# Two heads of a tile, issued in turn to the two halves of the TensorE array, in three attentions

## The chip, the cores and the metric

The kernel runs on one core of one Trainium2 chip. The metric is the device time of one execution in microseconds; the time of a kernel is the median of its runs. TensorE (PE in the profile, its weight loads PEld) does the matmuls and writes them to PSUM, which has eight banks of 128 partitions and 512 float32; VectorE (DVE) and ScalarE (ACT) do the elementwise work, GpSimd (POOL) a few powers, SyncE (SP) issues the DMAs. A matmul takes a stationary operand and a moving one; the rows of the array are the partitions over which it sums, the columns are the partitions of its output. A product over 64 partitions uses rows 0-63 or 64-127 of the array, a product with 64 outputs uses columns 0-63 or 64-127.

## What is computed

Three transformer blocks over 512 tokens of 1024 features, in float32, one after the other. Each has projections with large weights, and these hold most of the matmuls. The three attentions that the change touches have heads of 64 features, two of them in the two halves of a tile of 128 partitions:

```python
# block 1, differential attention: 4 heads, two score products each, values 128 wide
a = softmax(q1 k1^T / 8 + bias, causal) - lam * softmax(q2 k2^T / 8 + bias, causal)
out = a v
# block 2, stick-breaking attention: 16 heads of 64
z = q k^T / 8, masked                      # source s before target t
a[s, t] = exp(z[s, t] - sum over s <= u < t of softplus(z[u, t]))
out = a^T v
# block 3, forgetting attention: 8 heads of 64
a = softmax(q k^T / 8 + (cum[t] - cum[s]), causal);  out = a v
```

A fourth attention (block 2, two latent projections, heads of 128 + 64) and a chunked linear attention (block 1) are not touched.

## The kernel before, in words

Activations lie with features on partitions and tokens along the free dimension, a tile being 128 x 512. Projections are made of two float32r numbers an operand, three matmuls a row block (`mm`, L444 to L446; token-major `mm_tok`, L454 to L456), with weights that SyncE loads and ScalarE and VectorE split (`load`). PSUM has a pool of three banks for projections (`pm`) and five banks with roles: `ms` (1), `sc` (2, scores), `tr` (1, transposes), `po` (1, values). A scheduler orders each engine's instructions at build time: what stands first in the program goes first when its operands and a buffer are free; else something later goes ahead. `fill(n)` emits pieces of projection work queued in `fillers` between the steps of an attention, so that TensorE has work while a softmax runs. `later(f, depth)` holds back the value product of a block for `depth` further pieces.

- Differential attention (`diff_attention`): for each head and each block of 128 queries, from the last (512 keys) to the first (128 keys), two score products. `da_proj` has made of q and k, with `stack`, tiles of float32r numbers in which the high parts of one half head stand in its own 64 rows and the low (or again the high) ones in the other 64. `scores` (L423, L424) is one product over 128 rows and one over 64, at least 256 columns wide. Then the softmax of both, one `fill`, and `apply`: transposes, and values at L910.
- Stick breaking (`sb_pair`, eight calls): two heads, the same 64 rows of two tiles (`half`). Source blocks 1, 2, 3 are the first pass, block 0 the second. The five score banks hold blocks 1 and 3 of each head, block 2 of both, block 0 of each head. A product of 64 rows (L1164) is followed by its mask, an identity product over 128 rows in bfloat16 (L1165). Then per bank Abs, Exp, Ln on ScalarE and the split on VectorE and ScalarE; `fill(2)`; the sums over later source blocks (L1182 to L1186), Exp, and values (L1195) into 64 of the 128 output partitions a head. Groups of two calls share a set of five fillers, which the calls' four passes take by twos; the last group has eight gate projections.
- Forgetting attention (`fox_pair`, four calls): first all four query blocks of the head in rows 0-63, then those of the head in rows 64-127. A score product of 64 rows (L1724), its mask (L1725), the softmax, a `fill` at every second block, and `apply` held back by two blocks: transposes (L962), values (L1710) into the head's 64 output partitions. Twelve fillers of the last two calls include two idle turns.

Plain float32 products show as two matmul instructions each in the profile, the high and the low part of the stationary operand.

Of the kernel before, what the change touches and what calls it, by code (L numbers as in the profile page):

```python
# [9 lines left out]
F32 = mybir.dt.float32  # L10
F32R = mybir.dt.float32r
# [5 lines left out]
P = 128  # L17
# [11 lines left out]
# ---------------------------------------------------------------- host layout  # L29
# [201 lines left out]
# ---------------------------------------------------------------- the program  # L231


def idle():
    """a turn that a schedule leaves out"""


class Norm:
    """Takes the tiles of a stage's input as they become final: splits x * g and sums the squares."""
# [20 lines left out]
    def add_pe(self, k, x, sl):  # L260
        """the same with the sums over the tiles on the tensor engine"""
# [19 lines left out]
    def rows(self, sl, role):  # L281
        """the reciprocal root mean squares of some tokens, on all partitions, in PSUM"""
        rc = self.rstd(sl)
        return self.net.bcast_ps([rc[:, j:j + 1] for j in range((sl.stop - sl.start) // P)], role)


class Net:
# [83 lines left out]
    def fill(self, n=1):  # L371
        """emit n of the pieces of work queued to run beside the one at hand"""
# [12 lines left out]
    # ---- operands as sums of two float32r numbers  # L385
# [15 lines left out]
    def stack(self, src, twice, scale=None):  # L401
        """two heads of 64 rows as operands of products over 128 rows: a tile a head with its high parts in its
        own rows and, in the other 64, its low parts, or the high parts again and the low ones apart"""
        nc = self.nc
        tiles = [self.t(F32R, "st") for _ in range(2)]
        low = self.t(F32R, "lo") if twice else None
        for par, hl in enumerate(tiles):
            own, other = ROWS[par], ROWS[1 - par]
            if scale is None:
                nc.scalar.copy(hl[own], src[own])  # L410
                nc.vector.tensor_tensor((low[own] if twice else hl[other]), src[own], hl[own].bitcast(F32), ALU.subtract)
            else:
                nc.scalar.activation(hl[own], src[own], AF.Identity, bias=0.0, scale=scale)
                nc.vector.scalar_tensor_tensor(hl[other], src[own], scale, hl[own].bitcast(F32), ALU.mult, ALU.subtract)
            if twice:
                nc.scalar.copy(hl[other], src[own])
        return tiles, low

    def scores(self, out, a, ca, b, cb, par, start=True, stop=False, **k):
        """out (+)= a[:, ca]^T b[:, cb] of one of two stacked heads; one of a and b is stacked twice"""  # L420
        (at, al), (bt, bl) = a, b
        own = ROWS[par]
        self.nc.tensor.matmul(out, at[par][:, ca], bt[par][:, cb], start=start, stop=False, **k)  # L423
        self.nc.tensor.matmul(out, (al or at[par])[own, ca], (bl or bt[par])[own, cb], start=False, stop=stop, **k)  # L424
# [13 lines left out]
    def mm(self, out, w, c0, x, start=True, stop=True):  # L438
        """out[128 features, tokens] (+)= w[:, c0:c0+128]^T x"""
# [1348 lines left out]
```

## Time and profile before

| | us |
|---|---|
| median of 3 runs | 2565.46 |
| lowest and highest run | 2542.45 and 2569.28 |
| span of the profiled execution | 2572.3 |
| TensorE busy | 2522.8 |
| VectorE busy | 1320.8 |
| ScalarE busy | 1002.6 |
| mean granted TensorE clock | 0.979 |

The span runs from the first to the last instruction of the profiled execution. Busy shares are averages over stages with different limits. Matmuls are pipelined and the ends of their records are modelled, so what a matmul costs is read from its start to the start of the next one.

### The profile page before, as it was taken

Reading aid. Unit: us, or ns where it says so; the run is one execution under the profiler, and the core shown is the slowest. Engines: PE = TensorE matmul, PEld = TensorE weight load, DVE = VectorE, ACT = ScalarE, POOL = GpSimd, SP = SyncE. Lnnn points to the kernel's source line nnn. Section 1 sums busy time; section 2 is a strip of 40 time slices with the busy share of each in tenths; the row PEclk is TensorE's granted clock in tenths of the full one; section 3 lists DMA queues with packets and bytes.
Section 4 is the critical chain, followed back from the end, with each engine's and each line's share of the span. In section 5 each row is a group of like instructions: output and inputs, shape, how many; then the busy total and the mean of one; then the engine's idle time right before and its main releaser. Section 6 shows DMA issues by size and latency. Waiting matters only on the chain. (4 is left out here: it accounts for less than half of the span.)

```text
span 2572.3 us, 31426 instructions
## 1 busy us (share of the span) xinstructions
PE 2522.8 (98%) x12646; PEld 2025.7 (79%) x12646; DVE 1320.8 (51%) x2225; ACT 1002.6 (39%) x1586; POOL 63.5 (2%) x62
## 2 busy tenths in 40 slices
PE   8999999999999999999999999999999999999998
PEld 6857788888888877776777798888896768888887
DVE  7546556774775743345655664223362464532333
ACT  5434433442444445555323533232242444422221
POOL 0000000000000000000000000000010001000001
PEclk9999999999999999999999999999997999999999
DMA  5223235433434331122322123232221111322221
GB/s 189 92 77 96 87 100 179 140 118 120 155 109 131 115 96 59 65 67 73 119 69 83 34 74 110 87 107 98 90 73 51 62 50 42 98 94 96 98 88 52
DMA packets 71746, 240.78 MB, mean 94 GB/s; under 512 B 8232, under 2 KB 11184, under 8 KB 71600
## 3 DMA queue, kind: packets, MB, share of 16 engines
q1 hardware_dynamic: 71600, 238.78, 28.6%
q8 instruction: 99, 1.62, 0.3%
q14 instruction: 47, 0.39, 0.1%
HBM read 236.64 MB, written 2.11 MB: 93 GB/s over the span
## 5 line engine op out<-in xcount | busy, mean ns | idle before, releaser
L444 PE MATMUL pm<-hi,wh 128*128 128x512 f32 (+1 forms) x2736 | 1051.0, 385 | 8.8 <-ACT hi L390 5.0
L445 PE MATMUL pm<-lo,wh 128*128 128x512 f32 (+1 forms) x2736 | 1048.1, 383 | 0.0
L446 PE MATMUL pm<-hi,wl 128*128 128x512 f32 (+1 forms) x2736 | 1043.1, 382 | 0.0
L434 ACT CAST wh<-raw 128x1024 fp32r<-128x1024 f32 (+1 forms) x372 | 382.3, 1029 | 844.4 <-PE pm L445 582.0
L435 DVE TENSOR_TENSOR wl<-raw,wh 128x1024 fp32r<-128x1024 f32 (+1 forms) x372 | 445.1, 1197 | 491.2 <-ACT wh L434 468.6
L444 PEld LDWEIGHTS pm<-hi,wh 128*128 128x128 f32 x2736 | 519.6, 190 | 111.1 <-issue 9.0
L445 PEld LDWEIGHTS pm<-lo,wh 128*128 128x128 f32 x2736 | 519.6, 190 | 100.6 <-issue 7.9
L446 PEld LDWEIGHTS pm<-hi,wl 128*128 128x128 f32 x2736 | 519.3, 190 | 99.1 <-issue 5.5
L454 PE MATMUL pm<-wh,hi 128*128 128x256 f32 x400 | 118.8, 297 | 0.9 <-ACT vt L831 0.9
L456 PE MATMUL pm<-wh,lo 128*128 128x256 f32 x400 | 116.8, 292 | 0.0
L1403 DVE CUSTOM_DVE_ANT_0 adaw<-adaw,cb 128x1024 f32<-128x1024 f32 x72 | 88.0, 1222 | 55.5 <-DMA adaw<-in_w_ada 55.4
L455 PE MATMUL pm<-wl,hi 128*128 128x256 f32 x400 | 116.5, 291 | 0.0
L1482 DVE TENSOR_TENSOR sg<-sg,pm 128x512 f32<-128x512 f32 x44 | 30.2, 687 | 133.3 <-PE pm L446 133.3
L587 POOL TENSOR_TENSOR rc<-ms,nhalf 128x4 f32<-128x4 f32 (+2 forms) x29 | 39.4, 1357 | 2387.1 <-DVE ms L592 1811.1
L454 PEld LDWEIGHTS pm<-wh,hi 128*128 128x128 f32 x400 | 79.9, 200 | 6.4 <-issue 5.1
L456 PEld LDWEIGHTS pm<-wh,lo 128*128 128x128 f32 x400 | 79.8, 199 | 0.8 <-issue 0.6
L455 PEld LDWEIGHTS pm<-wl,hi 128*128 128x128 f32 x400 | 79.9, 200 | 0.6 <-issue 0.2
L496 PE MATMUL pm<-hi,wh 128*128 128x256 f32 (+1 forms) x216 | 61.6, 309 | 10.0 <-ACT hi L397 7.2
L985 DVE SCALAR_TENSOR_TENSOR uy<-ur,vec,uy 128x511 f32<-128x511 f32 x88 | 65.7, 748 | 9.0 <-ACT uy L983 8.0
L258 DVE TENSOR_TENSOR acc<-acc,sq 128x512 f32<-128x512 f32 (+1 forms) x93 | 54.8, 596 | 23.1 <-ACT sq L254 21.9
L498 PE MATMUL pm<-hi,wl 128*128 128x256 f32 (+1 forms) x216 | 66.4, 309 | 0.0
L497 PE MATMUL pm<-lo,wh 128*128 128x256 f32 (+1 forms) x216 | 66.3, 309 | 0.0
(352 smaller groups left out, 2488.4 us busy)
## 6 DMA issues: line engine op xcount, KB each, us to landing
raw<-in_w_gu SPq DMA_DIRECT2D x88, 512.0 KB, 3.4
adaw<-in_w_ada SPq DMA_DIRECT2D x72, 512.0 KB, 3.3
raw<-in_w_dn SPq DMA_DIRECT2D x48, 512.0 KB, 3.3
raw<-in_w_up SPq DMA_DIRECT2D x44, 512.0 KB, 3.3
raw<-in_w_g SPq DMA_DIRECT2D x16, 512.0 KB, 3.3
raw<-in_w_l0qk SPq DMA_DIRECT2D x16, 512.0 KB, 3.4
raw<-in_w_l SPq DMA_DIRECT2D x12, 512.0 KB, 3.4
X<-in_x SPq DMA_DIRECT2D x16, 256.0 KB, 5.8
```

Source lines behind the costliest of these rows:

```text
L434: nc.scalar.copy(wh[:, :n], raw[:, :n])
L435: nc.vector.tensor_tensor(wl[:, :n], raw[:, :n], wh[:, :n].bitcast(F32), ALU.subtract)
L444: self.nc.tensor.matmul(out, a, xh, start=start and k == 0, stop=False)
L445: self.nc.tensor.matmul(out, a, xl, start=False, stop=False)
L446: self.pe = self.nc.tensor.matmul(out, b, xh, start=False, stop=stop and k == n - 1)
L454: self.nc.tensor.matmul(out, xh[:, sl], a, start=start and k == 0, stop=False)
L455: self.nc.tensor.matmul(out, xh[:, sl], b, start=False, stop=False)
L456: self.pe = self.nc.tensor.matmul(out, xl[:, sl], a, start=False, stop=stop and k == len(x) - 1)
L497: self.nc.tensor.matmul(o[:, sl], wh[:, k], xl[:, sl], start=False, stop=False)
L498: self.nc.tensor.matmul(o[:, sl], wl[:, k], xh[:, sl], start=False, stop=k == 7)
L985: nc.vector.scalar_tensor_tensor(y[:, sh:], raw[:, :S - sh], self.v("fconv_w", 44 * (2 - sh) + f), y[:, sh:], mult, add)
L1403: nc.vector.tensor_tensor_reduce(w, w, cb, 0.5, 0.0, ALU.mult, ALU.add, mod[:, i:i + 1])
```

## The change

The two heads of one tile are now issued next to each other, one in rows 0-63 and one in rows 64-127, and their values one in columns 0-63 and one in columns 64-127. In the differential attention `stack` and `scores` go; q and k stay plain float32 tiles, and a score product is one float32 matmul over 64 rows, no wider than its keys. In stick breaking a call takes the two halves of one tile `c`; all products of a pass go out ahead of its masks, block by block and head by head, block 2 of the second head gets a bank of its own (role `ms`), so that Abs, the evacuation and Exp of that tile come in two halves, and the outputs of both heads are copied at once. In the forgetting attention the two heads run together: two score banks a query block, a `fill` at every block, the value products of a pair held back by one pair and issued key block by key block, head by head. Comments and docstrings are removed throughout.

```diff
@@ da_proj
-            y = self.q(F32, "dqk")
+            y = self.t(F32, "dqk")
...
-            (dk if i % 2 else dq).append(self.stack(y, i % 2 == 1))
+            (dk if i % 2 else dq).append(y)
@@ diff_attention
-                for a in range(2):
-                    ps = self.psa("das", "sc")
-                    w = max(n, 2 * P)
-                    self.scores(ps[:, :w], dq[h], slice(qb * P, n), dk[h], slice(0, w), a, stop=True)
+                sc = [self.psa("das", "sc") for _ in ROWS]
+                for ps, r in zip(sc, ROWS):
+                    nc.tensor.matmul(ps[:, :n], dq[h][r, qb * P:n], dk[h][r, :n], start=True, stop=True)
+                for a, ps in enumerate(sc):
@@ stick_breaking
-            for half in range(2):
-                last = self.sb_pair(*cur, half, o[2 * grp:2 * grp + 2], pre)
+            for c in range(2):
+                last = self.sb_pair(*cur, c, o[2 * grp + c], pre)
@@ sb_pair
-        members = [[(1, 0), (3, 0)], [(1, 1), (3, 1)], [(2, 0), (2, 1)], [(0, 0)], [(0, 1)]]
-        roles = ["sc", "sc", "tr", "sc", "sc"]
+        place = {(1, 0): (0, 0), (3, 0): (0, 384), (1, 1): (1, 0), (3, 1): (1, 384), (2, 0): (2, 0), (2, 1): (2, 256), (0, 0): (3, 0), (0, 1): (4, 0)}
+        bank = {(1, 0): (0, 0), (3, 0): (0, 384), (1, 1): (1, 0), (3, 1): (1, 384), (2, 0): (2, 0), (2, 1): (3, 0), (0, 0): (4, 0), (0, 1): (5, 0)}
+        parts = [[(0, slice(0, S))], [(1, slice(0, S))], [(2, slice(0, 256)), (3, slice(256, S))], [(4, slice(0, S))], [(5, slice(0, S))]]
+        roles = ["sc", "sc", "tr", "ms", "sc", "sc"]
...
-        for banks in ((0, 1, 2), (3, 4)):
-            for b in banks:
-                z[b] = self.psa("z", roles[b])
-                for i, (sb, par) in enumerate(members[b]):
-                    zr = reg(z, sb, par)
-                    nc.tensor.matmul(zr, k[par][r, sb * P:(sb + 1) * P], q[par][r, sb * P:], start=i == 0, stop=False, skip_group_check=True)
-                    nc.tensor.matmul(zr[:, 0:P], self.bf["ident"], self.bf["mask_sb"], start=False, stop=False, skip_group_check=True)
+        for tiles, blocks in (((0, 1, 2), (1, 2, 3)), ((3, 4), (0,))):
+            for t in tiles:
+                for b, _ in parts[t]:
+                    z[b] = self.psa("z", roles[b])
+            for sb in blocks:
+                for par, r in enumerate(ROWS):
+                    nc.tensor.matmul(zreg(sb, par), k[c][r, sb * P:(sb + 1) * P], q[c][r, sb * P:], start=sb < 3, stop=False, skip_group_check=True)
+            for t in tiles:
+                for sb, par in [m for m in place if place[m][0] == t]:
+                    nc.tensor.matmul(zreg(sb, par)[:, 0:P], self.bf["ident"], self.bf["mask_sb"], start=False, stop=False, skip_group_check=True)
                 e = self.t(F32, "sbe")
                 with self.tc.issue_after(pre.ins):
-                    nc.scalar.activation(e, z[b], AF.Abs)
+                    for b, sl in parts[t]:
+                        nc.scalar.activation(e[:, sl], z[b][:, width(sl)], AF.Abs)
...
-            for b in banks:
-                for sb, par in members[b]:
-                    col = (sb % 2) * 256 + (2 * par + half) * 64
-                    nc.tensor.matmul(po[64 * par:64 * par + 64, sb * P:], vt[sb // 2][:, col:col + 64], reg(pr, sb, par), start=sb == 1, stop=sb == 0, skip_group_check=True)
-        nc.vector.tensor_copy(out[0][r], po[0:64])
-        nc.scalar.copy(out[1][r], po[64:128])
+            for sb in blocks:
+                for par in range(2):
+                    col = (sb % 2) * 256 + (2 * c + par) * 64
+                    nc.tensor.matmul(po[ROWS[par], sb * P:], vt[sb // 2][:, col:col + 64], reg(pr, sb, par), start=sb == 1, stop=sb == 0, skip_group_check=True)
+        nc.vector.tensor_copy(out, po)
@@ fox_pair
-        def apply(p, qb, par, r):
+        def apply(ps, qb):
...
-            aT = self.transposed(p, qb)
+            aT = [self.transposed(p, qb) for p in ps]
             for kb in range(qb + 1):
-                col = (kb % 2) * 256 + (2 * cl + par) * 64
-                nc.tensor.matmul(po[0][r, qb * P:P * (qb + 1)], vt[kb // 2][:, col:col + 64], aT[:, kb * P:(kb + 1) * P], start=kb == 0, stop=kb == qb)
+                for par, r in enumerate(ROWS):
+                    col = (kb % 2) * 256 + (2 * cl + par) * 64
+                    nc.tensor.matmul(po[0][r, qb * P:P * (qb + 1)], vt[kb // 2][:, col:col + 64], aT[par][:, kb * P:(kb + 1) * P], start=kb == 0, stop=kb == qb)
...
-        for par in range(2):
-            h = 2 * c + par
-            r = slice(64 * par, 64 * par + 64)
-            cb = cum[h]
-            for qb in range(NB - 1, -1, -1):
-                n = P * (qb + 1)
-                ps = self.psa("fxs", "sc")
+        for qb in range(NB - 1, -1, -1):
+            n = P * (qb + 1)
+            sc = [self.psa("fxs", "sc") for _ in ROWS]
+            for ps, r in zip(sc, ROWS):
                 nc.tensor.matmul(ps[:, :n], q[r, qb * P:n], k[r, :n], start=True, stop=False)
+            for ps in sc:
                 nc.tensor.matmul(ps[:, qb * P:n], self.bf["ident"], self.bf["mask_q"], start=False, stop=True)
+            prob = []
+            for par, ps in enumerate(sc):
+                cb = cum[2 * c + par]
...
-                if qb % 2:
-                    self.fill()
-                self.later(lambda p=p, qb=qb, par=par, r=r: apply(p, qb, par, r), 2)
+                prob.append(p)
+            self.fill()
+            self.later(lambda p=prob, qb=qb: apply(p, qb), 1)
```

## Rows read from the trace of the kernel before

**Rows 1.** The page: span, then busy us, share and count of each engine.

```profile
span 2572.3 us, 31426 instructions
PE 2522.8 (98%) x12646; PEld 2025.7 (79%) x12646; DVE 1320.8 (51%) x2225; ACT 1002.6 (39%) x1586; POOL 63.5 (2%) x62
```

**Rows 2.** Windows: from:to, length, busy PE, PEld, DVE, ACT, POOL, clock, DMA, GB/s.

```profile
204.00:351.00 147.00, 146.43 (x689) 109.29 (x687) 90.75 (x237) 65.16 (x137) 6.78 (x4) 1.00 0.27 87
917.00:1203.00 286.00, 286.00 (x1415) 210.35 (x1414) 119.34 (x159) 157.13 (x249) 0.00 (x0) 0.95 0.21 70
1973.00:2137.00 164.00, 161.88 (x959) 119.58 (x959) 88.83 (x256) 72.62 (x152) 3.45 (x5) 1.00 0.18 57
```

**Rows 3.** Timeline, TensorE, stick breaking, first pass: start, length, instruction, count.

```profile
1097.17 0.91 PE L1164 MATMUL z<-sqk 64*128 64x384 f32 x2
1098.01 0.23 PE L1165 MATMUL z<-bf_mask_sb,bf_ident 128*128 128x128 bf16 x1
1098.17 0.48 PE L1164 MATMUL z<-sqk 64*128 64x128 f32 x2
1098.59 0.23 PE L1165 MATMUL z<-bf_mask_sb,bf_ident 128*128 128x128 bf16 x1
...
1101.78 0.36 PE L454 MATMUL pm<-wh,hi 128*128 128x256 f32 x1
```

**Rows 4.** Timeline, TensorE, stick breaking, second pass.

```profile
941.28 1.12 PE L1164 MATMUL z<-sqk 64*128 64x512 f32 x2
...
943.55 0.23 PE L1165 MATMUL z<-bf_mask_sb,bf_ident 128*128 128x128 bf16 x1
943.59 0.48 PE L444 MATMUL pm<-hi,wh 128*128 128x512 f32 x1
```

**Rows 5.** Timeline, TensorE: gating values of two column halves; forgetting values of one head.

```profile
2068.70 1.09 PE L1601 MATMUL sgu<-sw,sv 128*64 128x128 f32 x16
2069.73 0.44 PE L962 MATMUL tr<-cst,fxp 128*128 128x128 f32 x2
...
2081.28 1.09 PE L1710 MATMUL fxo<-aT,fvt 128*64 128x128 f32 x8
2082.29 0.33 PE L962 MATMUL tr<-cst,fxp 128*128 128x128 f32 x1
```

**Rows 6.** Timeline, TensorE, differential attention: two heads' scores of 512, 384, 256 columns.

```profile
279.75 0.48 PE L423 MATMUL das<-st 128*128 128x512 f32 x1
...
281.45 0.50 PE L444 MATMUL pm<-hi,wh 128*128 128x512 f32 x1
...
288.97 0.42 PE L423 MATMUL das<-st 128*128 128x384 f32 x1
...
290.43 0.50 PE L444 MATMUL pm<-hi,wh 128*128 128x512 f32 x1
...
298.31 0.36 PE L423 MATMUL das<-st 128*128 128x256 f32 x1
...
299.54 0.50 PE L444 MATMUL pm<-hi,wh 128*128 128x512 f32 x1
```

**Rows 7.** Timeline, TensorE, differential attention: scores of two heads with projections between.

```profile
323.00 0.42 PE L423 MATMUL das<-st 128*128 128x384 f32 x1
...
325.20 0.33 PE L423 MATMUL das<-st 128*128 128x384 f32 x1
```

**Rows 8.** Tile view of the stacked tiles: count, ns least/median/most, first and last start.

```profile
L410 ACT CAST st<-dqk x16: 602/616/622, 144.1 to 207.4; 64x512 fp32r<-64x512 f32 x16
```

**Rows 9.** Timeline, ScalarE, stick breaking: casts of two banks' high parts.

```profile
1055.85 0.62 ACT L390 CAST hi<-sbe 128x512 fp32r<-128x512 f32 x1 [0.76 <-DVE sbe L1171]
...
1059.05 0.62 ACT L390 CAST hi<-sbe 128x512 fp32r<-128x512 f32 x1 [0.76 <-DVE sbe L1171]
```

**Rows 10.** Windows at half the clock in stick breaking: the first, and all five summed.

```profile
921.30:928.10 6.80, 6.80 (x17) 4.42 (x18) 3.83 (x6) 3.42 (x6) 0.00 (x0) 0.50 0.54 175
sum 27.20, PE 27.20 PEld 19.78 DVE 12.55 ACT 16.75 POOL 0.00; mean PE 5.44 PEld 3.96 DVE 2.51 ACT 3.35 POOL 0.00
```

More of the change, by code (lines that the diff above doesn't have):

```diff
@@ L234, in idle @@
 def idle():
+    pass
 class Norm:
@@ L399, in split_scaled @@
         return h, l
[L401 to L424, printed above, removed]
     def load(self, name, u, kc, g):
@@ L1141, in stick_breaking, with sb_pair @@
         self.out_half("w_l0o", y, norm)
-    def sb_pair(self, q, k, vt, half, out, pre):
+    def sb_pair(self, q, k, vt, c, out, pre):
         nc = self.nc
-        r = slice(64 * half, 64 * half + 64)
-        place = {}
-        for par in range(2):
-            place[1, par] = (par, 0)
-            place[3, par] = (par, 384)
-            place[2, par] = (2, 256 * par)
-            place[0, par] = (3 + par, 0)
-        members = [[(1, 0), (3, 0)], [(1, 1), (3, 1)], [(2, 0), (2, 1)], [(0, 0)], [(0, 1)]]
-        roles = ["sc", "sc", "tr", "sc", "sc"]
-        z, sp, hi, lo, pr = ([None] * 5 for _ in range(5))
+        place = {(1, 0): (0, 0), (3, 0): (0, 384), (1, 1): (1, 0), (3, 1): (1, 384), (2, 0): (2, 0), (2, 1): (2, 256), (0, 0): (3, 0), (0, 1): (4, 0)}
+        bank = {(1, 0): (0, 0), (3, 0): (0, 384), (1, 1): (1, 0), (3, 1): (1, 384), (2, 0): (2, 0), (2, 1): (3, 0), (0, 0): (4, 0), (0, 1): (5, 0)}
+        parts = [[(0, slice(0, S))], [(1, slice(0, S))], [(2, slice(0, 256)), (3, slice(256, S))], [(4, slice(0, S))], [(5, slice(0, S))]]
+        roles = ["sc", "sc", "tr", "ms", "sc", "sc"]
+        sp, hi, lo, pr = ([None] * 5 for _ in range(4))
+        z = [None] * 6
@@ L1157, in sb_pair @@
         reg = lambda tiles, sb, par: tiles[place[sb, par][0]][:, place[sb, par][1]:place[sb, par][1] + S - sb * P]
+        zreg = lambda sb, par: z[bank[sb, par][0]][:, bank[sb, par][1]:bank[sb, par][1] + S - sb * P]
+        width = lambda sl: slice(0, sl.stop - sl.start)
         po, last = None, None
-        for banks in ((0, 1, 2), (3, 4)):
-            for b in banks:
-                z[b] = self.psa("z", roles[b])
-                for i, (sb, par) in enumerate(members[b]):
-                    zr = reg(z, sb, par)
-                    nc.tensor.matmul(zr, k[par][r, sb * P:(sb + 1) * P], q[par][r, sb * P:], start=i == 0, stop=False, skip_group_check=True)
-                    nc.tensor.matmul(zr[:, 0:P], self.bf["ident"], self.bf["mask_sb"], start=False, stop=False, skip_group_check=True)
+        for tiles, blocks in (((0, 1, 2), (1, 2, 3)), ((3, 4), (0,))):
[8 more added lines that the diff above has]
+                    nc.tensor.matmul(zreg(sb, par)[:, 0:P], self.bf["ident"], self.bf["mask_sb"], start=False, stop=False, skip_group_check=True)
@@ L1172, in sb_pair @@
-                sp[b] = e
-                hi[b], lo[b] = self.split(e)
+                for b, sl in parts[t]:
+                    nc.vector.scalar_tensor_tensor(e[:, sl], z[b][:, width(sl)], 0.0, e[:, sl], ALU.max, ALU.add)
+                sp[t] = e
+                hi[t], lo[t] = self.split(e)
             self.fill(2)
-            for b in banks:
-                for sb, par in members[b]:
-                    zr = reg(z, sb, par)
+            for t in tiles:
+                for sb, par in [m for m in place if place[m][0] == t]:
+                    zr = zreg(sb, par)
@@ L1186, in sb_pair @@
                             nc.tensor.matmul(dst, w, reg(lo, src, par), start=False, stop=done, skip_group_check=True)
-                pr[b] = self.t(F32, "sba")
+                pr[t] = self.t(F32, "sba")
                 with self.tc.issue_after(pre.ins):
-                    last = nc.scalar.activation(pr[b], z[b], AF.Exp)
+                    for b, sl in parts[t]:
+                        last = nc.scalar.activation(pr[t][:, sl], z[b][:, width(sl)], AF.Exp)
             if po is None:
                 po = self.psa("sbo", "po")
-            for b in banks:
-                for sb, par in members[b]:
-                    col = (sb % 2) * 256 + (2 * par + half) * 64
-                    nc.tensor.matmul(po[64 * par:64 * par + 64, sb * P:], vt[sb // 2][:, col:col + 64], reg(pr, sb, par), start=sb == 1, stop=sb == 0, skip_group_check=True)
-        nc.vector.tensor_copy(out[0][r], po[0:64])
-        nc.scalar.copy(out[1][r], po[64:128])
+            for sb in blocks:
[3 more added lines that the diff above has]
+        nc.vector.tensor_copy(out, po)
         return last
```

4 lines of the change are left out of this document (1 added, 3 removed).

## The prediction

> **What bounds the kernel now.** I read the page first, for its busy shares: TensorE is busy in 98% of a span of 2572.3 us, VectorE in 51%, ScalarE in 39% [rows 1]. Then the busy time by stretches, for the three attentions that the change touches: the differential attention (204 to 351 us), the stick-breaking attention (917 to 1203) and the forgetting attention (1973 to 2137). The reader is to see that TensorE is busy in all but 0.6, 0 and 2.1 us of them, while VectorE and ScalarE are busy in 42 to 62% and 44 to 55% [rows 2]. Projections queued as fillers run wherever an attention waits for its softmax. So a microsecond of TensorE work that goes is a microsecond of the kernel, as long as the fillers still cover the softmax. Then the order of time, TensorE alone, start to start, because busy times of pipelined matmuls overlap.
>
> **What one score product costs.** In the stick-breaking attention one head and one source block at a time uses 64 rows. 384 columns take 0.84 us until the mask starts, 128 columns take 0.42, and the mask 0.16 until the next product starts [rows 3]. So a product costs 1.64 ns a column ((0.84 - 0.42) / 256) and 0.21 us that do not depend on its length (0.42 - 128 x 1.64 ns): the first weights and the way out of the 64 rows. A mask ahead of a projection costs only 0.04 [rows 4]. One pass over three source blocks of two heads takes 4.61 us [rows 3], the pass over the last block 2.31 [rows 4]; the formula gives 6 x 0.21 + 1536 x 1.64 ns + 5 x 0.16 + 0.04 = 4.62 and 2.30.
>
> **What two halves of the array cost together.** The trace has no two neighbouring products in different rows, but it has them in different columns. Sixteen value products of the spatial gating, issued in turn to columns 0-63 and 64-127, take 1.03 us; eight products of the same 128 columns of data, all of one head of the forgetting attention, take 1.01 [rows 5]. Products in two column halves run wholly side by side, also as float32. For rows the gain is bounded by nothing (each head's stream after the other's) and by the same factor of two. I take two: the scores use separate banks for the two heads, as the new place table of stick breaking shows, and nothing in the column case pays for the second half. The Trainium skill, "TensorE: Matmul & The Clock Gate", section "Measured speedup vs the span model", states 3.07 for four row tiles of 32, not 4; the same share of the ideal would be an estimate of 1.54 for two. The streams below (67.2 us) would then shrink by 23.6 and not 33.6 us, and the time would be 10 us above mine.
>
> **Stick breaking, scores.** Eight calls. The first pass becomes one visit to the 64-row layout: 0.21 + (384 + 256 + 128) x 1.64 ns = 1.47 us, and six masks behind each other. The first of them costs up to 0.16, the others between 0.04 and 0.16; I take 0.4 in all, nearer the low end since no way in or out lies between them (0.24 to 0.96). 4.61 - 1.87 = 2.74. The second pass: 0.21 + 512 x 1.64 ns + two masks 0.2 = 1.25; 2.31 - 1.25 = 1.06. Eight times 3.80 is 30.4 us. At the three places where one group of heads follows another without fillers, the first head's bank comes free before the second's, so the blocks of 384 and 128 columns may go out one head at a time: minus 3 x (512 x 1.64 ns + 0.16) = 3.0. Left: 27.4. The values of the first pass are already issued in column pairs, and the last block's second head waits for its own exponential in either kernel: 0. The added halves of Abs, Exp and evacuation (block 2 now lies in two banks) are ScalarE and VectorE work under the fillers: 0 on the path.
>
> **Forgetting attention.** Before: 32 visits of 0.21 us and 4 pairs x 2 heads x 1280 columns. After: 16 visits, half the stream. 32 x 0.21 + 10240 x 1.64 ns = 23.5 becomes 16 x 0.21 + 5120 x 1.64 ns = 11.8 us, 11.7 less. The masks stay; the way into the 64 rows (0.16 - 0.04 = 0.12, what a mask costs more ahead of a product than ahead of a projection) is taken 16 times less: 1.9. Values: eight in a row take 1.01 us, and as sixteen in turn they take the same for both heads [rows 5]. The groups of a head have 8, 6, 4 and 2 products; at 0.11 a product and 0.15 fixed they cost 1.01, 0.80, 0.58 and 0.36, 2.75 a head, and one of two heads goes in each of four pairs: 11.0. Together 24.6. The transposes stay.
>
> **Differential attention.** The two products over stacked high and low parts become one float32 product a head. Before, two heads of 512, 384 and 256 columns take 1.70, 1.46 and 1.23 us, and the 128-column block is computed 256 wide at the price of 256 [rows 6]: 5.62 a head pair, 22.5 for four. After: 4 x (4 x 0.21 + 1280 x 1.64 ns) = 11.8, and the way into the 64 rows 16 times, 1.9: 8.8 less. In three of the 16 blocks the trace shows the second head 2.2 us behind the first, with projections between, because its bank came free later [rows 7]; there the streams do not meet, which takes back 3 x (384 x 1.64 ns + 0.33) = 2.9. Left: 5.9. The split into stacked tiles goes too: 24 casts of 0.62 us [rows 8] and 16 subtractions, on engines that nothing waited for: 0.
>
> **Where a wait could come.** Both score banks are now taken at once, and the next block's products wait for VectorE to read them. Behind them on TensorE stand the next fillers. In stick breaking one bank's chain to its high part takes 3.2 us (the casts of two banks lie 3.2 apart [rows 9]), so three banks and then two cost about 12 and 9 us a call with scores, exponential and values: 21 x 8 = 168 us against 286 - 27 = 259 us of TensorE work. It stays the bound. For single waits at passes without fillers of their own and at the two idle turns of the forgetting attention I take back 4 us (0 to 15).
>
> **The clock.** Five stretches of the stick-breaking attention, 27.2 us, ran at 0.50 of the clock, 1.2 instead of 2.4 GHz [rows 10]. Each begins within a pass of these 64-row products, one head at a time. That costs 13.6 us. Shorter passes with both halves at work should leave some of them out: I take 6 (-7 to +13.6).
>
> **Sum.** 27.4 + 24.6 + 5.9 - 4 + 6 = 59.9, that is 60 us. 2572.3 - 60 = 2512. The profiled span is 0.3% above the median of the runs (2565.46), so the prediction is 2565 - 60 = 2505 us.
>
> **The rivals.**
> 1. Rows do not overlap, only visits are saved. Stick breaking: 4.61 - (0.21 + 1536 x 1.64 ns + 0.4) = 1.48 and 2.31 - 2.09 = 0.22, times 8: 13.6. Forgetting scores: 3.4 + 1.9 = 5.3, values 11.0. Differential: 22.5 - (3.4 + 16.8 + 1.9) = 0.4. 30 - 4 = 26: 2539 us. For it: no row shows two row halves together; against it: the columns do.
> 2. The chain behind the scores becomes the limit: passes end sooner and fillers run out, so half the gain comes back as waits: 2535. For it: the stretches' fillers are uneven, one of four passes of a group has none of its own. Against it: the 168 us above. The Trainium skill, "TensorEngine Tiling (Array Packing)", section "PSUM Bottleneck", says that tiling speeds up TensorE and not the evacuation; no wait in these stretches shows that yet.
> 3. The order of issue does not survive: if the engine's queue keeps the heads apart as in [rows 7] everywhere, scores cost what they did, and the float32 products of the differential attention cost 32 x 0.33 + 16.8 - 22.5 = 4.9 more: 2570. Against it: only three of 16 blocks there are apart.
> 4. The other side: each of 48 paired steps (16 in each attention) leaves TensorE waiting for both banks. At 2.2 us, the distance in [rows 7] with nothing to fill it, that is 106 - 60 = 46 us more: 2611. It decides from 1.25 us a step (60 / 48). Against it: fillers stand behind nearly every step.
>
> **How the numbers follow.** Forecast 0.64, rival 1 0.13, rival 2 0.11, rival 3 0.05, rival 4 0.07. A change of over 1% (about what a measurement of this kernel can tell; its three runs span 27 us) begins below 2540. The forecast and half of rivals 1 and 2, which end near it, lie there, 0.76; the rest of those and rival 3 within 1%, 0.17; rival 4 above, 0.07. The likeliest case alone: all overlaps, no waits and the whole clock give 60 + 3 + 2.9 + 4 + 7.6 = 77.5 us, 2488; the clock worse by 13 and waits longer by 11 leave 36, 2529. With the scatter of the runs below and rivals 1 and 2 above: 2476 to 2545.
>
> **What would show it.** In the profile after: two score products of different heads starting within some 20 ns of each other; a first stick-breaking pass of about 1.9 us; value groups of the forgetting attention with twice the products in the same time; TensorE still busy throughout the three stretches, which get shorter by some 32, 24 and 6 us (stick breaking with its clock); fewer stretches at 0.50. Wrong it would be if products of different rows started one stream apart (rival 1), if TensorE waited for VectorE at the score banks (2, 4), or if projections stood between the heads (3).

## The result, and the profile after

The changed kernel takes 2527.89 us (median of 4 runs, 2511.96 to 2534.89) against 2556.64 us of the kernel before in the same rounds (4 runs, 2542.45 to 2569.28): ratio 0.9877, 95% interval 0.9832 to 0.9922. It is faster by 1.2%. In a later comparison it was 0.9833 (0.9804 to 0.9863). The predicted 2505 us was 23 us too low; the range, 2476 to 2545, held the time.

The page of the profile after (span; then busy us, share and count of each engine), against [rows 1]:

```profile
span 2510.2 us, 31392 instructions
PE 2456.1 (98%) x12646; PEld 1987.3 (79%) x12646; DVE 1310.9 (52%) x2217; ACT 981.3 (39%) x1570; POOL 62.8 (3%) x62
```

TensorE has lost 66.7 us of busy time with the same 12646 matmuls, and is still busy in 98% of the span. But the two spans, 2572.3 and 2510.2, must not be set against each other as they stand: the granted clock was 0.979 in the one and 0.991 in the other. **Span times mean granted clock** removes this. The four runs of the changed kernel have spans of 2510.2, 2532.3, 2519.9 and 2533.1 us at clocks of 0.991, 0.982, 0.987 and 0.982: the products are 2487.6, 2486.7, 2487.1 and 2487.5. The profile of before gives 2572.3 x 0.979 = 2518. So TensorE's work shrank by 31 us, and the other 31 us between the two profiles are clock. This product, called "at full clock" below, is the measure with which parts of 2 us can be seen. One run's product is rounded by up to 1.3 us, since the clock is given to three digits, and the products of one kernel scatter by some 1.7 us (standard deviation); a mean over four or more runs is good to about 1 us.

Windows of the three stretches after (from:to, length, busy PE, PEld, DVE, ACT, POOL, clock, DMA, GB/s), against [rows 2]:

```profile
208.00:349.00 141.00, 138.97 (x670) 101.83 (x669) 86.28 (x232) 58.86 (x126) 5.93 (x4) 1.00 0.26 85
918.00:1170.00 252.00, 251.63 (x1415) 193.23 (x1414) 119.63 (x167) 152.79 (x259) 0.00 (x0) 1.00 0.25 82
1914.00:2070.00 156.00, 149.37 (x940) 111.77 (x939) 88.16 (x255) 70.36 (x150) 3.46 (x5) 0.97 0.18 60
```

In stick breaking (second row) the same 1415 matmuls take 252 us instead of 286, TensorE is idle for no more than 0.4 us, and the clock is 1.00 instead of 0.95. In the forgetting attention (third row) TensorE is now idle for 6.6 us instead of 2.1, and the clock is 0.97 instead of 1.00.

Timeline of TensorE after (start, length, instruction, count), a first and a second pass of stick breaking, against [rows 3, 4]:

```profile
918.74 1.57 PE L1140 MATMUL z<-sqk 64*128 64x384 f32 x12
920.24 0.51 PE L1143 MATMUL z<-bf_mask_sb,bf_ident 128*128 128x128 bf16 x6
920.56 0.47 PE L419 MATMUL pm<-hi,wh 128*128 128x512 f32 x1
...
936.83 1.13 PE L1140 MATMUL z<-sqk 64*128 64x512 f32 x4
937.89 0.28 PE L1143 MATMUL z<-bf_mask_sb,bf_ident 128*128 128x128 bf16 x2
937.98 0.48 PE L419 MATMUL pm<-hi,wh 128*128 128x512 f32 x1
```

Start to start, the six products of a first pass take 1.50 us and their masks 0.32; before the same work took 4.61. The second pass takes 1.06 + 0.09 instead of 2.31. The tile view of the first 0.4 us of the first pass (count, ns least/median/most, first and last start, form) shows why: two matmuls, one of each head, begin at the same tenth of a microsecond (6 ns apart in the trace) and last 587 ns each, as long as the first matmul of one head alone did before.

```profile
L1140 PE MATMUL z<-sqk x2: 587/587/587, 918.7 to 918.7; 64*128 64x384 f32 x2
```

### The profile page after: what moved, and what is told of

Its sections match the earlier page's. It is cut to its first block, busy times and chain, and to the rows that moved or that the text cites. A ratio compares the mean times of both kernels' runs of the same rounds, so it can differ in the third digit from the quotient of the medians.

```text
span 2510.2 us, 31392 instructions
## 1 busy us (share of the span) xinstructions
PE 2456.1 (98%) x12646; PEld 1987.3 (79%) x12646; DVE 1310.9 (52%) x2217; ACT 981.3 (39%) x1570; POOL 62.8 (3%) x62
```

## The experiments

Every kernel was timed beside the kernel before, in the same rounds. "At full clock" is the mean over its runs. The versions of the last four rows are explained below.

By their times alone the versions with the changed stick breaking can hardly be told from each other: most of their intervals overlap. What follows on parts of a few microseconds rests on the products at full clock and on the traces.

| kernel | median us (runs) | ratio to before, 95% | at full clock, us |
|---|---|---|---|
| before, three comparisons | 2555.77 (13), 2562.97 (13), 2561.78 (11) | | 2519.3, 2517.8, 2518.7 |
| changed | 2527.89 (4) | 0.9877, 0.9832 to 0.9922 | 2487.2 |
| changed, again | 2517.47 (5) | 0.9833, 0.9804 to 0.9863 | 2488.4 |
| stick breaking alone | 2536.71 (4) | 0.9891, 0.9840 to 0.9941 | 2495.8 |
| forgetting attention alone | 2555.51 (10) | 0.9981, 0.9949 to 1.0014 | 2510.2 |
| differential attention alone | 2561.03 (10) | 1.0004, 0.9973 to 1.0036 | 2516.9 |
| score products head by head | 2524.91 (4) | 0.9861, 0.9806 to 0.9916 | 2487.8 |
| second transpose bank | 2530.31 (4) | 0.9880, 0.9828 to 0.9932 | 2479.9 |
| values one step later | 2512.19 (4), 2512.68 (6) | 0.9812, 0.9768 to 0.9857; 0.9812, 0.9771 to 0.9853 | 2475.5, 2474.2 |
| both | 2518.21 (4), 2501.70 (6) | 0.9816, 0.9757 to 0.9874; 0.9783, 0.9745 to 0.9821 | 2473.1, 2471.4 |
| both, without idle turns | 2518.49 (4) | 0.9820, 0.9768 to 0.9871 | 2473.5 |

**One part at a time.** Three kernels take the kernel before and one attention of the changed one. Stick breaking alone:

```diff
-            for half in range(2):
-                last = self.sb_pair(*cur, half, o[2 * grp:2 * grp + 2], pre)
+            for c in range(2):
+                last = self.sb_pair(*cur, c, o[2 * grp + c], pre)
```

> The kernel before, with the stick-breaking part of the change alone. I compare span times mean granted clock (time at full clock), which was 2518 us for the profiled run before and 2487 for each run after. Theory (the parts add up, each is TensorE time that goes): the score products and masks of stick breaking give 25 us, 3 to 4 come back in sums and values, so 2518 - 21.5 = 2497 us at full clock; the clock itself scatters from run to run between 0.980 and 0.991 as in both kernels. Rival (the clock is the gain): the clock stays above 0.990 in all runs, because the passes of single 64-row products are gone, and the median falls by 35 us.

Measured: 2495.8 us at full clock, 22.8 below the mean of before (2518.6), near the 21.5 of the theory. This is most of the whole gain. The clocks of its four runs, 0.983 to 0.991, exclude the rival.

The forgetting attention alone:

```diff
+        for qb in range(NB - 1, -1, -1):
...
+            sc = [self.psa("fxs", "sc") for _ in ROWS]
+            for ps, r in zip(sc, ROWS):
                 nc.tensor.matmul(ps[:, :n], q[r, qb * P:n], k[r, :n], start=True, stop=False)
```

> The kernel before, with the forgetting attention's part of the change alone. Theory: its scores and values give 12 us of TensorE time, of which 2 to 4 come back as transposes, masks and waits: 2518 - 8 = 2510 us at full clock (2507 to 2512). Rival (the differential attention's change gave the rest, this one nothing): 2518, the same as before.

Measured: 2510.2, only 8.4 below before, as expected after the profile, and a third of the 24.6 us predicted. The time itself can't be told from no change.

The differential attention alone:

```diff
...
-                    self.scores(ps[:, :w], dq[h], slice(qb * P, n), dk[h], slice(0, w), a, stop=True)
+                sc = [self.psa("das", "sc") for _ in ROWS]
+                for ps, r in zip(sc, ROWS):
+                    nc.tensor.matmul(ps[:, :n], dq[h][r, qb * P:n], dk[h][r, :n], start=True, stop=True)
```

> The kernel before with the differential attention of the changed kernel alone (one float32 product a head in 64 rows, two heads in turn, no stacked tiles). Theory (the three parts add, so the whole less the two others leaves this one 31.5 - 22.1 - 8.6 = 0.8 us): span times granted clock 2516 to 2518 us against 2518 of the kernel before; a ratio of 1.000 within 0.003. The scores themselves are some 5 us shorter from start to start, and transposes, rows brought to all partitions and projections take it back. Rival (the part is worth the 5.9 us of the prediction, and stick breaking or the forgetting attention lose 5 us in its company): 2512.

Measured: 2516.9, 1.7 below before. 22.8 + 8.4 + 1.7 = 32.9 against 30.7 of the whole (2518.6 less 2487.9, the mean of its nine runs): the parts add, within what the measure can tell, and the rival's loss of 5 us in company is not there.

**Is it the overlap?** In the changed kernel the order of the score products in a stick-breaking pass is turned back to one head after the other; nothing else moves:

```diff
-            for sb in blocks:
-                for par, r in enumerate(ROWS):
+            for par, r in enumerate(ROWS):
+                for sb in blocks:
                     nc.tensor.matmul(zreg(sb, par), ...
```

> The changed kernel with one thing undone: in each stick-breaking pass the three score products of head A are issued first and then the three of head B, instead of A and B in turn. Visits to the 64-row layout, masks behind each other, banks and everything else stay. Theory (the gain is the overlap of neighbours, and TensorE issues in order): only A's last block (128 columns) meets B's first (384); a first pass streams 384 + 256 + max(128, 384) + 256 + 128 = 1408 columns instead of 768, that is 640 x 1.64 ns = 1.05 us more, 8.4 us for the eight calls; the second pass has one block a head and stays. The scores of stick breaking go from 26 to about 34 us; span times granted clock 2495 us instead of 2487. Rival 1 (what paid was the single visit and the masks put together, not the overlap, or the engine finds the pairs itself): nothing changes, first pass 1.8 us, 2487. Rival 2 (rows would overlap even less once the order is broken: all of one head before the other): 768 columns more, 1.26 us a pass, 10 us, 2497.

Measured: 2487.8 at full clock, no difference that can be told in the runs; in the two traces the whole stick-breaking stretch, start to start, is 2.5 us longer (256.9 against 254.5). The passes show something between the theory and rival 1. Timeline of TensorE in this kernel, a pass over three source blocks and one over two:

```profile
916.76 2.32 PE L1140 MATMUL z<-sqk 64*128 64x384 f32 x12
919.01 0.51 PE L1143 MATMUL z<-bf_mask_sb,bf_ident 128*128 128x128 bf16 x6
...
981.00 1.14 PE L1140 MATMUL z<-sqk 64*128 64x384 f32 x8
982.08 0.40 PE L1143 MATMUL z<-bf_mask_sb,bf_ident 128*128 128x128 bf16 x4
```

The pass over three blocks is 2.25 us instead of 1.50; only four of the eight first passes go out in one piece, so this is 3.0 us in all (start to start the scores are 29.1 us instead of 26.1). The pass over two blocks (384 and 128 columns of one head, then of the other) takes 1.08 us, the same as in turn. In the built program all of head A's products of a pass stand ahead of head B's, as written. So products of head B start ahead of products of head A that were issued before them. The tile view of the first 0.75 and 0.84 us of the long pass (count, ns least/median/most, first and last start, forms) shows it:

```profile
L1140 PE MATMUL z<-sqk x3: 376/482/587, 916.8 to 917.5; 64*128 64x384 f32 x2, 64*128 64x256 f32 x1
L1140 PE MATMUL z<-sqk x4: 376/534/587, 916.8 to 917.5; 64*128 64x384 f32 x3, 64*128 64x256 f32 x1
```

A float32 product appears as two matmuls. The order of issue is A 384, 384, 256, 256, 128, 128, then B 384; but the fourth to start, 6 ns behind the first 256 of A, is a third 384: head B's, three matmuls of A ahead of their turn. So strict order, on which the theory's 8.4 us rested, is wrong; overlap is right, because a pass that had none would be 1.26 us longer (rival 2) and this one is 0.75. That the gain came from visits and masks alone is excluded by the pass over two blocks: its 1024 columns at 1.64 ns would take 1.68 us one behind the other. How far ahead B starts differs: with one product of A in between, in the pass over two blocks, B's first starts 13 ns behind A's first; with two in between, in the long pass, it starts 755 ns behind it, together with A's second product.

**Where the forgetting attention's gain went.** Timeline of TensorE in the changed kernel, at the change from one pair of heads to the next:

```profile
1953.41 0.38 PE L937 MATMUL tr<-cst,fxp 128*128 128x128 f32 x2
1953.72 1.12 PE L1702 MATMUL fxs<-fqk 64*128 64x512 f32 x2
1954.77 0.44 PE L937 MATMUL tr<-cst,fxp 128*128 128x128 f32 x2
1955.14 0.43 PE L1691 MATMUL fxo<-aT,fvt 128*64 128x128 f32 x2
1955.50 1.12 PE L1702 MATMUL fxs<-fqk 64*128 64x512 f32 x2
1956.55 0.65 PE L1691 MATMUL fxo<-aT,fvt 128*64 128x128 f32 x6
1957.14 0.28 PE L1704 MATMUL fxs<-bf_mask_q,bf_ident 128*128 128x128 bf16 x2
```

The first head's probabilities are transposed (1953.41), and the second head's must wait until ScalarE has copied them out of the one bank of the role "tr". Into this gap the order of instructions puts what is ready: one head's scores alone (1953.72), and the first value product alone (1955.14), whose partner needs the second copy. Then the other head's scores go alone too (1955.50). In 6 of the 16 score pairs the heads are apart, in four of them with transposes in between like this, and most value groups begin with a single product (two matmuls). Two cures were made. The first puts the values one step later: `self.side` holds work that is done in the next step, behind its transposes.

```diff
         def apply(ps, qb):
+            aT = [self.transposed(p, qb) for p in ps]
+            self.side.append(lambda: values(aT, qb))
+
+        def values(aT, qb):
             if not po:
                 po.append(self.psa("fxo", "po"))
-            aT = [self.transposed(p, qb) for p in ps]
             for kb in range(qb + 1):
```

> The kernel after, but in the forgetting attention the value products of a pair follow one step behind its transposes instead of right behind them. Theory (one transpose bank: the second head's transposes wait for ScalarE to copy the first head's, and single products go out in that gap): the score pairs meet in 15 of 16 blocks instead of 10, values lose the single first products; score products 16.7 to about 12.5 us, values 16.7 to about 12, at full clock 2487 - 9 = 2478 us. Rival (the score banks: the second bank comes free later than the first): the pairs stay apart where they were, 2487 us.

Measured: 2475.5 at full clock, and 2474.2 in a second comparison, beside the changed kernel (2488.4): 12 to 14 us better, with the single bank still in place. The heads are together in 15 of 16 score pairs, as the theory said.

> The version with the values of the forgetting attention one step behind the transposes, beside the changed kernel. Theory (what held the forgetting attention is gone): span times granted clock 2477 +- 2 us in every run, 10 us below the changed kernel; ratio to the kernel before 0.981 to 0.985 against 0.986 to 0.990 of the changed kernel. Rival (the 10 us are an accident of single runs): no difference between the two.

A bank for the second head's transposes, alone:

```diff
-    def transposed(self, p, qb):
+    def transposed(self, p, qb, role="tr"):
...
-        ps = self.psa("tr", "tr")
+        ps = self.psa("tr", role)
...
-            aT = [self.transposed(p, qb) for p in ps]
+            aT = [self.transposed(p, qb, role) for p, role in zip(ps, ("tr", "ms"))]
```

> The changed kernel with one thing altered: in the forgetting attention the second head's probabilities are transposed into a PSUM bank of their own (another role's bank, free at that time), so that they need not wait until ScalarE has copied the first head's out. The values stay where they were, right behind the transposes. Theory (the single transpose bank is what keeps the heads' products apart): most of what the version with the values one step later gained comes by the bank alone, span times granted clock 2478 to 2481 us, against 2487 of the changed kernel and 2477 of that version; start to start scores fall from 16.7 to about 14 us, values from 16.7 to about 14, transposes from 14.1 to about 11. Rival (the place of the values is what counts: they wait for the second copy in any case, and single products of other steps are issued in that gap): 2485 to 2488, with scores and values near 16.7.

Measured: 2479.9, 8 us better, as the theory said. Its details were not: six score pairs are apart as before, which is the rival's point, the scores fell only to 16.2 us, and the transposes, in which a wait of 2.1 us for the copy now lies, stayed at 13.9. The values fell to 14.5 as expected, and the masks from 6.6 to 2.3; in the changed kernel a wait of 3.2 us for the copy lay in them.

Both together, and both without the two idle turns:

> The changed kernel with both cures in the forgetting attention: the second head's transposes in their own bank, and the values one step behind the transposes; the order of fillers stays, with its two idle turns. Theory (both cures take away the same gap): no better than the values' place alone, 2474 to 2478 us in span times granted clock. Rival (each takes away a gap of its own): their gains add, 2468 to 2471. Its difference from the version that also leaves out the idle turns (2474) shows what those turns are worth: within 2 us.

> The version with both cures, beside the two others. Theory (they take away the same gap but for some 4 us): span times granted clock 2472 +- 2 us, ratio to the kernel before 0.979 to 0.983, the lowest of the three. Rival (the second bank gives nothing beyond the values' place): 2477, as the version without it.

```diff
-                self.fillers = [gates[0], idle, gates[1], idle, *gates[2:]]
+                self.fillers = [*gates]
```

> The kernel after, with three edits in the forgetting attention: the second head's transposes go to a bank of their own (role ms), the values follow one step behind, and the fillers of the last two calls lose their two idle turns, so that the branch products stand beside the last blocks. Theory (transposes in one bank plus a tail without fillers): as with the values behind, and of the 6 us of single waits in this stretch half goes too: 2487 - 13 = 2474 us at full clock, median about 2514. Rival (VectorE and ScalarE bound the tail): no better than with the values behind alone, 2478.

Measured: 2473.1 and 2471.4 with both, 2473.5 without the idle turns. The second bank adds 2 to 3 us to the values' place, between the theory and its rival, so the cures take away nearly the same gap. What was expected of leaving out the idle turns is not there: they are worth nothing that can be told. The ratios of the second comparison came out at or below the low end of what was expected (0.9833, 0.9812 and 0.9783). The same change of pairs with both cures, timeline of TensorE:

```profile
1957.69 0.38 PE L937 MATMUL tr<-cst,fxp 128*128 128x128 f32 x2
1958.00 0.87 PE L1694 MATMUL fxo<-aT,fvt 128*64 128x128 f32 x10
1958.80 1.13 PE L1705 MATMUL fxs<-fqk 64*128 64x512 f32 x4
1959.86 0.28 PE L1707 MATMUL fxs<-bf_mask_q,bf_ident 128*128 128x128 bf16 x2
```

The scores of both heads now stand in one row (x4) and take 1.06 us from start to start, where they took 1.05 twice; ten value matmuls go together in 0.80. One of 16 pairs is still apart. The ledger of the stretch, TensorE start to start at full clock, from the first score product to the product behind the last value product; a wait counts for the instruction before it:

| us | before | changed | second bank | values later | both |
|---|---|---|---|---|---|
| scores | 23.5 | 16.7 | 16.2 | 13.8 | 12.2 |
| values | 22.1 | 16.7 | 14.5 | 13.9 | 13.8 |
| transposes | 11.6 | 14.1 | 13.9 | 11.9 | 13.5 |
| masks | 4.5 | 6.6 | 2.3 | 3.8 | 2.1 |
| projections and the rest | 99.2 | 96.2 | 94.9 | 93.2 | 94.7 |
| whole stretch | 160.9 | 150.2 | 141.8 | 136.6 | 136.2 |

With both cures the kernel is 0.9783 (0.9745 to 0.9821) of the kernel before, 2501.70 us in the comparison where the changed kernel took 2517.47 and the one before 2561.78. It is the best version found, though its interval and that of the changed kernel there (0.9804 to 0.9863) still touch.

> The changed kernel once more, beside the two versions with a cure, on one chip in the same rounds. Theory (a kernel's work at full clock is fixed, and the granted clock scatters from run to run): span times granted clock of every run within 2487 +- 2 us, the clock anywhere from 0.979 to 0.992, median 2515 to 2535 us. Rival (the changed kernel holds the clock better than the kernel before, so that part of its gain comes from there): its mean clock over the runs lies above that of the kernel before by more than 0.002.

**The clock.** Measured: products of 2486.3 to 2490.5, a little wider than expected, at clocks of 0.985 to 0.991. Within this comparison the clock went the rival's way, 0.9888 in the mean against 0.9839 of the kernel before; in the first four runs of the changed kernel it was 0.9855, and 0.9853 and 0.9873 in the two kernels beside it here. Over all later comparisons and these four runs, 45 runs with the changed stick breaking had a mean clock of 0.9856, 57 runs without it 0.9845; both sets scatter from 0.979 to 0.992. The difference is worth 3 us, with a 95% interval from 1 us lost to 7 us won, so the time does not show whether the change wins any clock. The 13 kept profiles show where it could. Windows at half the clock: inside stick breaking, one of three and the sum of the three, in each of the two other kernels with the old stick breaking (differential alone, then forgetting alone); and one at L1624, in the kernel before:

```profile
1028.70:1032.10 3.40, 3.40 (x15) 2.76 (x15) 1.58 (x3) 2.38 (x4) 0.00 (x0) 0.50 0.00 0
sum 10.20, PE 10.20 PEld 8.43 DVE 5.74 ACT 7.33 POOL 0.00; mean PE 3.40 PEld 2.81 DVE 1.91 ACT 2.44 POOL 0.00
963.80:970.60 6.80, 6.80 (x29) 5.59 (x28) 3.04 (x5) 4.85 (x9) 0.00 (x0) 0.50 0.00 0
sum 17.00, PE 17.00 PEld 13.57 DVE 8.42 ACT 10.56 POOL 0.00; mean PE 5.67 PEld 4.52 DVE 2.81 ACT 3.52 POOL 0.00
1931.70:1965.80 34.10, 33.95 (x70) 17.25 (x71) 3.04 (x4) 6.22 (x10) 0.00 (x0) 0.50 0.09 31
```

All three profiles with the old stick breaking have 10 to 27 us at 0.50 inside it [rows 10]; of the ten with the new one none has any there. In the profiles this is 5 to 14 us of clock that the change wins in this stretch. But most of the scatter lies elsewhere: 7 of the 13 profiles, with either stick breaking, have a stretch of 31 or 34 us at 0.50 that starts about where the products of L1624 do, which spread the gate sums to all partitions just ahead of the forgetting attention. The change does not touch them. The stretch costs 15 to 17 us, half of what the clock's range from 0.979 to 0.992 is worth. The 31 us of clock between the profiles of before and after are these two: 13.6 from stick breaking and 17 from L1624. All other half-clock stretches sum to 49 us in each.

## Why the prediction was right or wrong

The sign and the mechanism were right, the size was not: without its 6 us for the clock the sum says 54 us, and 31 were measured at full clock. Heads that the order of work keeps apart are what the sum priced too low: the prediction had this as rival 3, at 0.05 and as all or nothing, and allowed for three places in stick breaking, three in the differential attention and none in the forgetting attention; the trace has four, five and six. By the number alone rival 1, at 2539 us, was nearer to the 2528 measured than the forecast, but its mechanism is excluded. Term by term:

- **Overlap of rows: right.** Rival 1 predicted a first pass 1.48 us shorter; it is 2.79 shorter (4.61 to 1.82, predicted 1.87). Its scores take 1.50 us, 1.47 by the full factor of two. The Trainium skill, "TensorE: Matmul & The Clock Gate", section "Measured speedup vs the span model", has 3.07 for four row tiles of 32; the same share of the ideal, an estimate of 1.54 for two, would make them 0.21 + 1536 x 1.64 ns / 1.54 = 1.85 us, which this trace does not show.
- **Stick breaking: 27.4 predicted, 22.8 measured.** Scores and masks fell from 54.8 to 29.7 us (28.0 predicted). Three second passes and one first pass have their heads apart, where a group of heads follows another; three were allowed for. Sums, values and projections became 1.6, 0.9 and 1.1 us longer, which the prediction left out or had at nothing. Why is not shown. The way into the 64 rows, 0.12 us a visit, explains little of it: an instruction other than a mask stands ahead of 22 visits now and stood ahead of 19 of 64 before.
- **Forgetting attention: 24.6 predicted, 8.4 measured.** This is the step that failed: "16 visits, half the stream", and for values "as sixteen in turn they take the same for both heads". Both counted pairs as written in the program. The order on TensorE puts whatever is ready into a wait, and a step had such a wait between its two heads: the second head's transposes wait for the copy out of the one bank, and the values behind them for both copies. Either cure takes most of it away, so it is this wait and not the bank alone. The prediction wrote "the transposes stay": it counted their time and not their bank. Of the evacuation it wrote that no wait in these stretches shows it yet; but the waits of TensorE before have one there, of the values for the copy of the transposes (line, waited for, total, times, longest):

```profile
PE fxo L1710 <- ACT aT L964: 1.2, 1, 1.2
```

  With both cures the stretch is 24.7 us shorter than before (160.9 to 136.2), close to the term, but this is in part luck. The scores gave 11.3 of 11.7 us and the masks 2.4 of 1.9; the values gave 8.3 of 11.0, the transposes became 1.9 longer, and 4.5 lie in projections and the rest. Of these, some 2 come back behind the stretch, which holds ten projection matmuls fewer, at 0.23 us; so it is in the changed kernel's stretch, with nine fewer.
- **Differential attention: 5.9 predicted, 1.7 measured.** The scores themselves fell by 5.4 us (21.8 to 16.4). But five of 16 blocks have the heads apart, not three, and transposes, broadcasts, values and reversals became 3.0 us longer. In the kernel with this part alone the projections became 1.0 us longer, and TensorE waits 1.0 us in this stretch for a DMA, where it waited for none before. The way into the 64 rows was priced at 1.9 us; that the 3.0 are this way is not shown. Timeline of TensorE after, one block with the heads together and one with them apart:

```profile
278.71 1.13 PE L913 MATMUL das<-dqk 64*128 64x512 f32 x4
279.77 0.49 PE L885 MATMUL dao<-aT,vt 128*128 128x128 f32 x2
...
288.41 0.91 PE L913 MATMUL das<-dqk 64*128 64x384 f32 x2
289.25 0.50 PE L421 MATMUL pm<-hi,wl 128*128 128x512 f32 x1
...
291.30 0.91 PE L913 MATMUL das<-dqk 64*128 64x384 f32 x2
292.14 0.50 PE L420 MATMUL pm<-lo,wh 128*128 128x512 f32 x1
```

  Together, 512 columns of two heads take 1.06 us instead of 1.70 [rows 6]. Apart, 384 columns take 0.84 twice, 1.68 us instead of 1.46: such a block is slower than before, because the product over stacked parts that it replaces was cheaper than two float32 products that do not meet. The two stand 2.9 us apart; in [rows 7] it was 2.2. The prediction took that distance for all three such blocks of before; in the two others it was 1.3 and 1.2 us, and a fourth block had transposes between its heads.
- **Waits: 4 predicted, 4 found**, in the forgetting attention (waits of 2.2 us before, 6.5 after), nearly all at its end and not in its midst; the differential attention has 1.4 more, for a DMA. The waits of TensorE between 2036 and 2070 us:

```profile
PE tr L937 <- ACT aT L939: 3.2, 1, 3.2
PE pm L419 <- ACT hi L390: 2.0, 1, 2.0
PE bc L574 <- POOL rc L562: 1.0, 1, 1.0
```

  The first is the transpose bank again, once its fillers are gone. Timelines of the two engines in the changed kernel at that place (in brackets: idle before it, and what ended it):

```profile
2042.61 0.57 ACT L1489 ACTIVATE ge<-pm 128x512 f32<-128x512 f32 x1
2045.15 0.63 ACT L1492 ACTIVATE ge<-ge 128x512 f32<-128x512 f32 x1 [1.97 <-DVE ge L1491]
2045.68 0.57 ACT L939 COPY aT<-tr 128x512 f32<-128x512 f32 x1
2046.31 0.73 PE L937 MATMUL tr<-cst,fxp 128*128 128x128 f32 x4 [3.21 <-ACT aT L939]
```

  The copy that would free the bank stands behind a function of the gate on ScalarE, which itself waits 1.97 us for VectorE. The Trainium skill, "TensorEngine Tiling (Array Packing)", section "PSUM Bottleneck", says that tiling makes TensorE faster and not what empties its banks. This trace has that wait, with the 3.21 us, though ScalarE was held up by VectorE and not by its own speed. Rival 2 was right in kind, at 4 us instead of 30.
- **The clock: 6 us predicted; 5 to 14 in the stretch, not shown in the time** (3 us, between -1 and 7). The half-clock stretches of stick breaking [rows 10] came back in all three profiles with the old passes and are gone in all ten with the new ones; but the time does not show it, since the clock varies from run to run by as much as the whole change is worth (0.979 to 0.992 of 2520 us is 33 us). The profile after also has half-clock stretches where the one before has none, the first right behind the wait above:

```profile
2046.80:2050.20 3.40, 3.34 (x21) 2.35 (x19) 2.42 (x10) 2.09 (x6) 0.00 (x0) 0.50 0.03 5
2053.60:2057.00 3.40, 3.40 (x17) 2.51 (x18) 0.45 (x2) 2.29 (x6) 0.00 (x0) 0.50 0.00 0
```

- **The base.** The prediction stood on 2565 us, a median of three runs; in the later comparisons before had medians of 2556 to 2563. That base, 2 to 10 us too high, made the forecast's miss smaller than that of its sum, which is luck. That the profiled execution after took 2512 us, just what the sum gives without the correction to the median, is chance: it ran at 0.991.

## What to carry to other kernels

Two heads in two halves of the array rows cost what one costs, but only where both are ready together: before counting the half, look at what each operand and each bank waits for, a single bank between the heads above all, and price the fraction of pairs that the order will keep apart. Where a kernel's products take turns, put the work that depends on a copied bank one step behind it; here this was worth 12 to 14 us, beside 31 of the change. On a bound engine with a scattering clock, compare span times granted clock, and look for a stretch at half the clock in several profiles before counting on it: here those in stick breaking came back in all three profiles of the old code, and a larger one elsewhere came and went with no change of code.

## What was not expected of the hardware

- Two float32 matmuls of 64 rows in the two halves overlap wholly: starts 6 ns apart, 587 ns each, and a pass of 2 x 768 columns takes 1.50 us where the formula for one head alone gives 1.47.
- TensorE does not keep to the order of issue across the halves: a matmul of the second half began while three matmuls of the first half issued before it had not begun, and 384 and 128 columns head by head (1.08 us) cost as much as in turn (1.07). With three products a head the order does matter: 2.25 us a pass head by head, 1.50 in turn.
- Work at full clock scatters by about 2 us in 2500 (the mean of before on three chips: 2517.8 to 2519.3), while the time scatters by 1%. Much of that 1% is one stretch of 31 or 34 us that ran at 0.50 in 7 of 13 profiles and at 1.00 in the others.
